# A written order for the start of a transformer layer, V weights a trip earlier, and one mixed tile on other engines

## The chip, the cores and the metric

The kernel runs on one core of one Trainium2 chip. TensorE (PE in the profile) multiplies matrices, ScalarE (ACT), VectorE (DVE) and GpSimd (POOL) work elementwise, and SyncE (SP) issues most of the transfers. The metric is the device time of one execution in microseconds (us), lower is better, compared as medians of several runs.

## The reference, cut to what matters

One decoder layer on x (1024 x 1024, float32). The change touches the first lines, where the groups' projection is made, and a split of the mixed result.

```
h = rms_norm(x, norm_mix_pre)
proj = h @ w_in                     # 1024 x 2816: u, v (256 each), q, k, vb (768 each)
a_out = spatial_gating(u, v, ...)   # gelu, LayerNorm of v in 4 groups, 128x128 causal w_s per group
b_out = dilated_attention(q, k, vb) # 12 heads
x = x + rms_norm(concat(a_out, b_out) @ w_out, norm_mix_post)
x = x + rms_norm(conv_gated_mlp(rms_norm(x, norm_ffn_pre)), norm_ffn_post)
```

## The kernel before, in words

All matmuls are made in pairs of reduced-precision parts. `split` (L71) copies a float32 block into a high part (`hi`, on ScalarE, VectorE or POOL) and subtracts that from the block to get the low part (`lo`); a product is then three matmuls: high by high, high by low, low by high.

The stages follow each other: the uv stage (normalise x, transpose it, project it on the u and v columns and gate), the V stage (projection on the attention's V columns in two halves, v0 and v1), the attention with 12 heads, the output projection, and the gated MLP.

The uv stage is a loop over eight tiles of 128 tokens (L329), here called trips 0 to 7. Its parts:

- `load_x` (L177) and `load_w` (L184) issue transfers on SP. x has two buffers, so the load of tile i+2 waits until tile i is normalised. The V weights use the two buffers called raw (L122), which `rows` and `spr` hold first.
- `norm_x` (L199): ScalarE squares a tile with a running sum (L212), POOL makes the mean `n_m` and the reciprocal root `n_r` (L145, L147), VectorE multiplies into `xn` (L214). Tile 0 goes in two halves, and takes the gain `g1` from two PSUM banks, into which TensorE spreads its one row (L253); the later tiles take it from `g1t` in SBUF, a copy by ScalarE (L259).
- `trans_x` (L217): TensorE transposes eight 128 x 128 blocks of `xn` into two PSUM banks; from each, ScalarE makes two high parts hTh and VectorE two low parts hTl.
- `split_w` (L190) splits a block of weights, `whuv`, `wluv` for u and v, and `whv`, `wlv` for V.
- `proj_a` (L234): 24 matmuls for a tile, three for each of eight blocks k. After k = 3 (after k = 5 for tile 0) it calls `mid`, which transposes the next tile, and finishes parts of earlier tiles.
- the gate in pieces, so that a tile's gate is spread over three trips: `uv_a` (L289: two Gelu on ScalarE; sum, mean, difference on VectorE; square on POOL, L300), `uv_b` (L302: sum of squares `s` on VectorE, `ln_m` and `ln_r` on POOL), `uv_c` (L308: product with `ln_r` on VectorE, product and sum with the gains `lnt` on POOL, L311, L312), `uv_d` (L314: split into vnh on ScalarE and vnl on VectorE).
- at the end of trip 1, `trans_rows` (L271) transposes `rows`; at the end of trip 2, `spatial_prep` (L320) masks `spr` on POOL (L321), transposes it on TensorE into spT (L325), and copies it to `wT`.

What sets the order: TensorE and SP issue their instructions as the code is written (`tc.manual_schedule(engines={ET.PE, ET.SP})`, L92). For ScalarE, VectorE and POOL a planner with a model of costs chooses the order at build time. In trip i the code has, in this order: `norm_x(i + 2)`, `load_x(i + 3)`, in trips 3 to 6 a load and a split of V weights (L342 to L344, low part on POOL), `proj_a(i)` with `mid` inside (`trans_x(i + 1)`, `uv_b(i - 1)`, `uv_d(i - 2)`), `uv_a(i)`, `uv_c(i - 1)`, and then the two preparations.

In the attention, `qk_row` (L510) makes the scores of 128 queries: TensorE, VectorE (L523), ScalarE's Exp (L528), a reciprocal `rz` (L530), and POOL's scaling of the row (L531). `tpv` (L538) transposes rows, splits them into pth (ScalarE) and ptl (VectorE, L556), and multiplies by V (L573). `load_qk` (L447) splits a head's weights, the low part wql on POOL. In the last head but one, `mix_split` (L614) splits seven blocks of the first tile of the mixed result, called `ms`, for the output projection: blocks with odd k by ScalarE and POOL, those with even k by VectorE alone.

Of the kernel before, what the change touches and what calls it, by code (L numbers as in the profile page):

```python
# [62 lines left out]
def build(tc, x, g1, g2, g3, g4, w_in, ln_g, ln_b, sp_w, sp_b, rel, w_out, w_gate, w_up,  # L63
# [7 lines left out]
    def split(hi, lo, src, hi_eng, lo_eng):  # L71
        if hi_eng is act:
            act.activation(hi, src, AF.Copy)  # L73
        elif hi_eng is pool:
            pool.tensor_scalar(hi, src, 1.0, None, op0=OP.mult)
        else:
            dve.tensor_copy(hi, src)
        lo_eng.tensor_sub(lo, src, hi.bitcast(F))  # L78
# [10 lines left out]
    def close_pool(key):  # L89
        cms.pop(key).__exit__(None, None, None)  # L90

    with tc.manual_schedule(engines={ET.PE, ET.SP}), \  # L92
# [17 lines left out]
        def bO(nm):  # L110
            return bank("O", 1, nm)
# [7 lines left out]
        def mtile(nm, dt=F):  # L119
            return mp.tile([128, 1024], dt, tag="M", name=nm)  # L120
# [8 lines left out]
        make_identity(nc, ident)  # L129
        half = cp.tile([128, 1], F, name="half")  # L130
        pool.memset(half, -0.5)
        ones = cp.tile([1, 128], F, name="ones")
        pool.memset(ones, 1.0)
        rows = raw("rows")
# [42 lines left out]
        def load_x(i):  # L177
            xt = sxp.tile([128, D], F, tag="x", name="x%d" % i)
            w = 512 if i == 0 else D
            for c in range(0, D, w):  # L180
                sp.dma_start(xt[:, c:c + w], x[i * 128:(i + 1) * 128, c:c + w])
            XT[i] = xt

        def load_w(key, c0, n, kp):  # L184
            r = mtile("r%d" % kp) if key == "uv" else raw("w%s%d" % (key, kp))
            v = r[:, :2 * n].rearrange("p (k c) -> p k c", k=2)
            sp.dma_start(v, w_in[kp * 256:(kp + 1) * 256, c0:c0 + n].rearrange("(k p) c -> p k c", p=128))
            RAW[key, kp] = v
# [25 lines left out]
                dve.scalar_tensor_tensor(xn, xt, r, g1t, op0=OP.mult, op1=OP.mult)  # L214
            XT[i] = xn

        def trans_x(i):  # L217
            if i == 0:
                for hf in range(2):
                    for kp in range(4):  # L220
                        for w in range(2):
                            hT[hf, kp, w] = htile("hT%s%d_%d" % ("hl"[w], hf, kp)).rearrange("p (k c) -> p k c", k=2)
            xn = XT[i]
            for q in range(2):
                p = bS("xT%d_%d" % (i, q))
                for k in range(4):
                    pe.transpose(p[:, k * 128:(k + 1) * 128], xn[:, (4 * q + k) * 128:(4 * q + k + 1) * 128], ident)
                s = slice((i % 4) * 128, (i % 4 + 1) * 128)
                for j in range(2):
                    pv = p[:, j * 256:(j + 1) * 256].rearrange("p (k c) -> p k c", k=2)  # L230
                    hi, lo = hT[i // 4, 2 * q + j, 0][:, :, s], hT[i // 4, 2 * q + j, 1][:, :, s]
                    split(hi, lo, pv, act, dve)

        def proj_a(key, n, i, nm, mid=None):  # L234
            p = bD(nm)
# [8 lines left out]
                pe.matmul(p[:, :n], hTv(i, k, 1), wh, start=False, stop=k == KT - 1)  # L244
            return p

        g1t, g1r = mtile("g1t"), mtile("g1r")
        load_x(0)
        sp.dma_start(g1r[0:1, :], bass.AP(tensor=g1.tensor, offset=g1.offset, ap=[[D, 1], [1, D]]))
        G1 = [bP("g1_%d" % hf) for hf in range(2)]  # L250
        for hf in range(2):
            s = slice(hf * 512, (hf + 1) * 512)
            pe.matmul(G1[hf], ones, g1r[0:1, s], start=True, stop=True)  # L253
        for kp in range(4):
            load_w("uv", 0, 512, kp)
        load_x(1)
        norm_x(0)
        for hf in range(2):
            act.activation(g1t[:, hf * 512:(hf + 1) * 512], G1[hf], AF.Copy)  # L259
        split_w("uv", 512, 0, dve, dve)  # L260
        trans_x(0)
        for kp in range(1, 4):
            split_w("uv", 512, kp, act if kp % 2 else dve, dve)

        def load_rows():
            sp.dma_start(rows[0:66, 0:128], conv_w.rearrange("k (f p) -> (k f) p", p=128))
# [53 lines left out]
        def spatial_prep():  # L320
# [5 lines left out]
            act.activation(wT[:, 0:512], p, AF.Copy)  # L326
            dve.tensor_sub(wT[:, 512:1024], p, wT.bitcast(F)[:, 0:512])

        for i in range(NT):  # L329
            if i == 0:  # L330
                load_x(2)
                norm_x(1)
            if i + 2 < NT:
                norm_x(i + 2)
            if i + 3 < NT:
                load_x(i + 3)
            if i == 0:
                sp.dma_start(lnt[:, 0:256], bcast(ln_g, 256))
                sp.dma_start(lnt[:, 256:512], bcast(ln_b, 256))
                sp.dma_start(sprv, sp_w.rearrange("g t s -> t g s"))  # L340
                load_rows()
            if i in (3, 4, 5, 6):  # L342
                load_w("v0", C0["v"], 384, i - 3)
                split_w("v0", 384, i - 3, act, pool)  # L344
            def mid():
                if i + 1 < NT:
                    trans_x(i + 1)
                if i >= 1:
                    uv_b(i - 1)
                if i >= 2:  # L350
                    uv_d(i - 2)

            p = proj_a("uv", 512, i, "uv%d" % i, mid)
            uv_a(i, p)
            if i >= 1:
                uv_c(i - 1)
            if i == 1:
                trans_rows()
            if i == 2:
                spatial_prep()  # L360
        close_pool("sx")

        BB = []
# [247 lines left out]
                split(wh[:, s], wl[:, s], r[:, s], ENG[WO_HI[k]], ENG[WO_LO[k]])  # L611
            WO.append((wh, wl))

        def mix_split(i, mh, ml, ks):  # L614
            s = slice(i * 128, (i + 1) * 128)
            for k in ks:
                src = mixT[k][:, s]
                split(mh[:, k], ml[:, k], src, act if k % 2 else dve, pool if k % 2 else dve)
            MS[i] = (mh, ml)

        YP = {}
# [18 lines left out]
        for h in range(HEADS):  # L640
            if h + 1 < HEADS:
                load_bias(h + 1)
            if h + 2 < HEADS:
                load_qk(h + 2)
            if h + 3 < HEADS:
                bias_copies(h + 3)
            if h == HEADS - 1:
                pump(len(fill))
                fill.extend(wout_mm(0, range(KT - 1), bD))
            for g in range(4):  # L650
                if g < 3:
                    qk_group(h, g + 1)
                elif h + 1 < HEADS:
                    qk_group(h + 1, 0)
                if h == HEADS - 2:
                    if g == 0:
                        m0 = [mtile("ms0_%d" % s, R).rearrange("p (k c) -> p k c", k=KT) for s in range(2)]
                        mix_split(0, m0[0], m0[1], range(KT - 1))
                    for k in WO_AT[g]:
                        load_wo(k)  # L660
                if h == 0 and g == 0:
                    pump(FILL_FIRST)
                last_pv()
                last_pv = tpv(h, g, FILL_AT.get(h, FILL)[g])
                if g == 3 and h + 2 < HEADS:
                    fill.extend(proj_qk(h + 2))
                if g == 3 and h == HEADS - 2:
                    pump(len(fill))
                    for k in WO_AT[4]:
                        load_wo(k)  # L670
# [586 lines left out]
```

## Time and profile before

| what | value |
|---|---|
| runs | 1202.24, 1201.06, 1197.48 us; median 1201.06 |
| the profiled execution's own time | 1199.82 us |
| its span, first to last instruction | 1198.1 us |
| mean granted TensorE clock | 0.992 of full speed |
| uv stage's last matmul issued | 71.46 us |
| first matmul of the V stage | 71.69 us |

In the rows of the profile, a line begins with its start and its length in us, or with a source line; then follow engine, operation, and out<-in by the program's names, the shape, and in brackets the idle time ahead of it and what ended that. `x4` is a count of instructions. A group's line ends with its busy time in us, the mean of one in ns, and the idle time before it. In the table of windows, the clock is the share of full speed that was granted to TensorE; at 0.50 its matmuls take twice the time.

### The profile page before, as it was taken

Reading aid. Unit: us, or ns where it says so; the run is one execution under the profiler, and the core shown is the slowest. Engines: PE = TensorE matmul, PEld = TensorE weight load, DVE = VectorE, ACT = ScalarE, POOL = GpSimd, SP = SyncE. Lnnn points to the kernel's source line nnn. Section 1 sums busy time; section 2 is a strip of 40 time slices with the busy share of each in tenths; the row PEclk is TensorE's granted clock in tenths of the full one; section 3 lists DMA queues with packets and bytes.
Section 4 is the critical chain, followed back from the end, with each engine's and each line's share of the span. In section 5 each row is a group of like instructions: output and inputs, shape, how many; then the busy total and the mean of one; then the engine's idle time right before and its main releaser. Section 6 shows DMA issues by size and latency. Waiting matters only on the chain.

```text
span 1198.1 us, 16554 instructions
## 1 busy us (share of the span) xinstructions
PE 1163.6 (97%) x5691; PEld 976.8 (82%) x5691; DVE 839.7 (70%) x1559; ACT 582.9 (49%) x1174; POOL 370.6 (31%) x402
## 2 busy tenths in 40 slices
PE   7899999999999999999999999999999999999996
PEld 5789978888887878887788888888888888888884
DVE  5752257777777775468997678777777679779665
ACT  5532256667765664457534243432434345446521
POOL 2850023334323374234033313332133310000451
PEclk9999999999999999999999999999999999999998
DMA  5323133343233442251143323433143289334345
GB/s 180 106 59 89 25 83 73 91 117 84 73 78 76 108 141 71 92 173 53 36 132 97 115 67 117 132 97 106 62 132 106 88 302 357 97 97 129 110 130 203
DMA packets 107420, 134.31 MB, mean 112 GB/s; under 512 B 30779, under 2 KB 74311, under 8 KB 107336
## 3 DMA queue, kind: packets, MB, share of 16 engines
q1 hardware_dynamic: 105032, 131.15, 35.9%
q10 hardware_dynamic: 2304, 2.10, 0.5%
q8 instruction: 45, 0.74, 0.3%
q14 instruction: 39, 0.32, 0.1%
HBM read 98.30 MB, written 35.71 MB: 112 GB/s over the span
## 4 chain that ended last, share of the span: by engine, by line
PE 86%; DVE 5%; DMA 3%; POOL 2%; ACT 2%; issue 2%; SPq 0%; DVEq 0%; POOLq 0%; ACTq 0%
PE d L996 15%; PE qk L479 10%; PE y L630 7%; PE o L573 4%; PE pt L551 4%; PE s L519 2%; PE s L520 2%; PE v L242 2%; PE v L244 2%; PE v L243 2%; PE Bu L857 2%; PE Au L856 2%; PE Au L857 2%; PE Au L855 2%; PE Bu L856 2%; PE Bu L855 2%
## 5 line engine op out<-in xcount | busy, mean ns | idle before, releaser
L996 PE MATMUL d<-t,s 128*128 128x512 f32 x924 | 211.9, 391 | 1.9 <-ACT t L73 1.6
L996 PEld LDWEIGHTS d<-t,s 128*128 128x128 f32 x924 | 174.5, 189 | 39.2 <-ACT t L73 2.0
L531 POOL TENSOR_SCALAR row<-row,rz 128x128 f32<-128x128 f32 (+3 forms) x96 | 72.8, 759 | 213.2 <-DVE rz L530 200.2
L528 ACT ACTIVATE row<-row,nm 128x128 f32<-128x128 f32 (+3 forms) x96 | 74.4, 775 | 49.0 <-DVE nm L523 48.7
L556 DVE TENSOR_TENSOR ptl<-pt,pth 128x512 fp32r<-128x512 f32 (+1 forms) x120 | 75.7, 634 | 19.6 <-ACT pth L555 18.3
L630 PE MATMUL y<-woh,ms 128*128 128x512 f32 x256 | 82.8, 396 | 0.4 <-DVE Q L494 0.4
L555 ACT ACTIVATE pth<-pt 128x512 fp32r<-128x512 f32 (+1 forms) x120 | 65.8, 550 | 33.3 <-PE pt L551 31.9
L479 PE MATMUL qk<-hTh,wqh 128*128 128x512 f32 x192 | 81.1, 422 | 0.0
L73 ACT ACTIVATE s<-sf 128x512 fp32r<-128x512 f32 x77 | 48.2, 626 | 65.7 <-PE d L996 26.4
L479 PE MATMUL qk<-hTl,wqh 128*128 128x512 f32 x192 | 78.7, 410 | 0.0
L479 PE MATMUL qk<-hTh,wql 128*128 128x512 f32 x192 | 76.6, 399 | 0.0
L78 DVE TENSOR_TENSOR s<-sf,s 128x512 fp32r<-128x512 f32 x77 | 53.5, 695 | 24.0 <-ACT s L73 23.9
L551 PE MATMUL pt<-ident,row 128*128 128x128 f32 x432 | 68.4, 274 | 1.6 <-POOL row L531 1.5
L1011 POOL TENSOR_TENSOR x<-x,g4t 128x512 f32<-128x512 f32 x12 | 18.4, 1536 | 158.0 <-DMA g4t<-in_norm_ffn_post 133.8
L73 ACT ACTIVATE wtg<-tg 128x512 fp32r<-128x512 f32 x44 | 27.5, 632 | 80.9 <-PE Cu L857 67.8
L805 POOL TENSOR_TENSOR tu<-wu 128x512 f32<-128x512 f32 x11 | 17.5, 1590 | 156.1 <-PE Ag L857 74.5
L908 DVE SCALAR_TENSOR_TENSOR c<-G,cols,c 128x1023 f32<-128x1023 f32 (+1 forms) x44 | 57.7, 1329 | 6.7 <-ACT c L906 6.7
L523 DVE CUSTOM_DVE_ANT_0 row<-s,bias 128x384 f32<-128x384 f32 (+2 forms) x96 | 49.9, 519 | 17.7 <-PE s L520 11.8
L551 PEld LDWEIGHTS pt<-ident,row 128*128 128x128 f32 x432 | 51.3, 140 | 10.4 <-POOL row L531 2.5
L73 ACT ACTIVATE wtu<-tu 128x512 fp32r<-128x512 f32 x44 | 27.6, 630 | 64.2 <-PE Cg L857 50.8
L630 PEld LDWEIGHTS y<-woh,ms 128*128 128x128 f32 x256 | 47.9, 188 | 10.8 <-issue 0.8
L573 PE MATMUL o<-ptl,V 128*128 128x256 f32 x240 | 49.4, 287 | 4.8 <-DVE ptl L556 4.5
(329 smaller groups left out, 3232.5 us busy)
## 6 DMA issues: line engine op xcount, KB each, us to landing
sf<-sD SPq DMA_DIRECT2D x77, 256.0 KB, 2.8
wu<-in_w_up SPq DMA_DIRECT2D x11, 1024.0 KB, 5.0
wd<-in_w_down SPq DMA_DIRECT2D x22, 512.0 KB, 7.0
wg<-in_w_gate SPq DMA_DIRECT2D x10, 1024.0 KB, 6.0
sD<-c SPq DMA_DIRECT2D x30, 256.0 KB, 6.5
gcop<-gd SPq DMA_DIRECT2D x12, 576.0 KB, 4.8
wqk<-in_w_in SPq DMA_DIRECT2D x24, 256.0 KB, 6.0
bias<-gcop SPq DMA_DIRECT2D x12, 512.0 KB, 4.1
```

The costliest lines, as they stand in the source:

```text
L73: act.activation(hi, src, AF.Copy)
L78: lo_eng.tensor_sub(lo, src, hi.bitcast(F))
L479: pe.matmul(st[hf], w, m, start=k == 0 and j == 0, stop=k == KT - 1 and j == 2)
L528: act.activation(t[:, :w], t[:, :w], AF.Exp, bias=nm, scale=-1.0, accum_out=z)
L531: pool.tensor_scalar(t[:, :w], t[:, :w], rz, 1.0, op0=OP.mult, op1=OP.mult)
L551: pe.transpose(p[:, a * 128:(a + 1) * 128], r[:, jj * 128:(jj + 1) * 128], ident)
L555: act.activation(hi[:, :n], p[:, :n], AF.Copy)
L556: dve.tensor_sub(lo[:, :n], p[:, :n], hi.bitcast(F)[:, :n])
L573: pe.matmul(ov, v, t[:, s], start=j == 0 and x == 0, stop=x == 1 and j == 2 * g + 1, skip_group_check=True)
L630: pe.matmul(YP[i, hf], m, w, start=k == 0 and j == 0, stop=k == KT - 1 and j == 2)
L908: dve.scalar_tensor_tensor(c[:, d:T], g[:, 0:T - d], col(2 - d, f), c[:, d:T], op0=OP.mult, op1=OP.add)
L996: pe.matmul(b, l, r, start=first and n in FIRST and q == 0, stop=last and n in LAST and q == 2, skip_group_check=True)
```

## The change

Five things are changed.

1. From the first loads to the end of the uv loop, ScalarE, VectorE and POOL are put under a written order as well: each issues its instructions as the code has them.
2. The start is written anew for that: the gain's row is loaded from ScalarE's queue, ahead of x; the four weight loads and the load of tile 1 come directly behind the load of tile 0; the first tile's normalisation comes ahead of the first weight split; the weight splits have ScalarE for all high parts, and the second of them stands between the two halves of the first tile's transposes; the copies of the gain come after the third; `norm_x(1)` moves up from trip 0.
3. TensorE multiplies a tile of zeros three times ahead of the gain's matmuls (`wz`, cleared by VectorE, into the bank `bO`).
4. The V weights are loaded in trips 2 to 5. They are split at the end of `mid` in trips 3, 4, 6 and 7, the low part on POOL in trips 3 and 4 and on VectorE in trips 6 and 7.
5. The seven blocks of the first mixed tile are all split by ScalarE and POOL.

```
+        wz = cp.tile([128, 256], F, name="wz")
+        dve.memset(wz, 0.0)
...
-        def trans_x(i):
+        def trans_x(i, mid=None):
...
+                if q == 0 and mid is not None:
+                    mid()
...
+        order = tc.manual_schedule(engines={ET.DVE, ET.Activation, ET.Pool})
+        order.__enter__()
         g1t, g1r = mtile("g1t"), mtile("g1r")
+        wb = bO("wb")
+        act.dma_start(g1r[0:1, :], bass.AP(tensor=g1.tensor, offset=g1.offset, ap=[[D, 1], [1, D]]))
         load_x(0)
-        sp.dma_start(g1r[0:1, :], bass.AP(tensor=g1.tensor, offset=g1.offset, ap=[[D, 1], [1, D]]))
+        for kp in range(4):
+            load_w("uv", 0, 512, kp)
+        load_x(1)
+
+        for _ in range(3):
+            pe.matmul(wb[:, :256], wz[:, :128], wz, start=True, stop=True)
         G1 = [bP("g1_%d" % hf) for hf in range(2)]
...
-        for kp in range(4):
-            load_w("uv", 0, 512, kp)
-        load_x(1)
         norm_x(0)
+        split_w("uv", 512, 0, act, dve)
+
+        def rest():
+            split_w("uv", 512, 1, act, dve)
+
+        trans_x(0, rest)
+        split_w("uv", 512, 2, act, dve)
         for hf in range(2):
             act.activation(g1t[:, hf * 512:(hf + 1) * 512], G1[hf], AF.Copy)
-        split_w("uv", 512, 0, dve, dve)
-        trans_x(0)
-        for kp in range(1, 4):
-            split_w("uv", 512, kp, act if kp % 2 else dve, dve)
+        split_w("uv", 512, 3, act, dve)
+        norm_x(1)
...
+        V0 = {3: 0, 4: 1, 6: 2, 7: 3}
         for i in range(NT):
             if i == 0:
                 load_x(2)
-                norm_x(1)
...
-            if i in (3, 4, 5, 6):
-                load_w("v0", C0["v"], 384, i - 3)
-                split_w("v0", 384, i - 3, act, pool)
+            if i in (2, 3, 4, 5):
+                load_w("v0", C0["v"], 384, i - 2)
             def mid():
...
+                if i in V0:
+                    split_w("v0", 384, V0[i], act, pool if i < 5 else dve)
...
+        order.__exit__(None, None, None)
         close_pool("sx")
...
-        def mix_split(i, mh, ml, ks):
+        def mix_split(i, mh, ml, ks, engs=None):
...
-                split(mh[:, k], ml[:, k], src, act if k % 2 else dve, pool if k % 2 else dve)
+                split(mh[:, k], ml[:, k], src, *(engs or ((act, pool) if k % 2 else (dve, dve))))
...
-                        mix_split(0, m0[0], m0[1], range(KT - 1))
+                        mix_split(0, m0[0], m0[1], range(KT - 1), (act, pool))
```

## The prediction

> **What bounds the kernel now.** I read the page's busy shares first, then the chain that ended last.
>
> ```profile
> PE 1163.6 (97%) x5691; PEld 976.8 (82%) x5691; DVE 839.7 (70%) x1559; ACT 582.9 (49%) x1174; POOL 370.6 (31%) x402
> PE 86%; DVE 5%; DMA 3%; POOL 2%; ACT 2%; issue 2%; SPq 0%; DVEq 0%; POOLq 0%; ACTq 0%
> ```
>
> TensorE is busy 97% of the span and carries 86% of the chain, so a change that leaves its matmuls alone can only move the places where it waits or runs at a lower clock. The table by windows shows two such places that the change touches (columns: stretch, its length, busy time of PE, PEld, DVE, ACT, POOL, then the granted clock):
>
> ```profile
> 41.42:47.91 6.49, 6.49 (x33) 5.34 (x32) 3.58 (x9) 4.48 (x11) 5.18 (x8) 1.00 0.61 203
> 47.91:51.86 3.95, 0.64 (x4) 0.19 (x2) 3.54 (x4) 0.70 (x3) 3.79 (x4) 1.00 0.14 23
> 53.12:56.53 3.41, 3.41 (x12) 2.81 (x11) 2.01 (x5) 1.93 (x4) 3.24 (x7) 0.50 0.01 2
> 56.53:71.69 15.16, 15.16 (x72) 12.36 (x71) 9.72 (x23) 5.02 (x15) 11.73 (x15) 1.00 0.23 67
> 367.40:370.57 3.17, 0.50 (x3) 0.50 (x4) 2.69 (x4) 1.55 (x4) 2.18 (x3) 1.00 0.14 31
> 370.57:373.97 3.40, 3.40 (x12) 2.82 (x11) 1.71 (x6) 0.59 (x1) 0.59 (x1) 0.50 0.05 11
> ```
>
> The first row is one dense trip of the uv loop, a projection and eight transposes: 6.5 us. In the second and the fifth TensorE stands (3.95-0.64 = 3.3 us, and 2.7 us), and soon after each it runs 3.4 us at half clock, which costs 3.4 x 0.5 = 1.7 us. The stalls are thus worth 5.0 and 4.4 us. After the second stretch the uv stage is dense to its end at 71.69 us (15.16 of 15.16). The timeline shows what made both stalls:
>
> ```profile
> 48.32 2.82 DVE L214 SCALAR_TENSOR_TENSOR xn<-x,n_6r,g1t 128x1024 f32<-128x1024 f32 x1 [0.49 <-ACT whv L73]
> 48.25 1.80 POOL L78 TENSOR_TENSOR wlv<-wv,whv 128x768 fp32r<-128x768 f32 x1
> 366.58 2.84 DVE L78 TENSOR_TENSOR ms<-mix,ms 128x128 fp32r<-128x128 f32 x3
> 366.62 2.65 POOL L78 TENSOR_TENSOR wql<-wqk,wqh 128x512 fp32r<-128x512 f32 x2 [0.17 <-ACT wqh L73]
> 370.07 0.50 PE L573 MATMUL o<-ptl,V 128*128 128x256 f32 x2 [2.68 <-DVE ptl L556]
> ```
>
> [...]
>
> **The change, step by step.** The V-weight splits go behind the transposes and later by an iteration, so 5.0 us of stall may go; the mixed tile leaves VectorE, so 4.4 us may go. But ScalarE, VectorE and POOL, which a planner orders now, get the order in which the code is written, and that order has to be followed through the loop. The rows for one trip:
>
> ```profile
> 33.22 1.28 DVE L214 SCALAR_TENSOR_TENSOR xn<-x,n_4r,g1t 128x1024 f32<-128x1024 f32 x1 [0.39 <-POOL n_4r L147]
> 39.93 1.28 DVE L214 SCALAR_TENSOR_TENSOR xn<-x,n_5r,g1t 128x1024 f32<-128x1024 f32 x1 [0.39 <-POOL n_5r L147]
> 39.02 0.25 POOL L145 TENSOR_SCALAR n_5m<-ss 128x1 f32<-128x1 f32 x1
> 39.35 0.55 POOL L147 TENSOR_TENSOR n_5r<-n_5m,half 128x1 f32<-128x1 f32 x1
> L78 DVE TENSOR_TENSOR hTl<-xT,hTh 128x256 fp32r<-128x256 f32 x28 | 11.0, 417 | 3.0 <-ACT hTh L73 2.7
> L73 ACT ACTIVATE hTh<-xT 128x256 fp32r<-128x256 f32 x28 | 10.1, 381 | 17.2 <-DVE hTl L78 11.1 <-PE xT L227 6.0
> 71.46 0.39 PE L244 MATMUL uv<-whuv,hTl 128*128 128x512 f32 x1
> 70.62 0.43 DVE L310 TENSOR_TENSOR tm<-tm,ln6r 128x256 f32<-128x256 f32 x1 [1.42 <-POOL ln6r L147]
> 71.13 0.73 POOL L311 TENSOR_TENSOR tm<-tm,lnt 128x256 f32<-128x256 f32 x1 [0.54 <-DVE tm L310]
> 71.94 0.74 POOL L312 TENSOR_TENSOR tm<-tm,lnt 128x256 f32<-128x256 f32 x1
> 73.53 0.73 POOL L300 TENSOR_TENSOR tm<-tm 128x256 f32<-128x256 f32 x1 [0.85 <-DVE tm L299]
> 74.29 0.42 DVE L305 TENSOR_REDUCE s<-tm 128x4 f32<-128x256 f32 x1 [0.51 <-POOL tm L300]
> 74.80 0.19 POOL L145 TENSOR_SCALAR ln7m<-s 128x4 f32<-128x4 f32 x1 [0.54 <-DVE s L305]
> 75.07 1.02 POOL L147 TENSOR_TENSOR ln7r<-ln7m,half 128x4 f32<-128x4 f32 x1
> 24.69 0.74 POOL L321 TENSOR_SCALAR_AFFINE_SELECT spr<-spr 128x512 f32<-128x512 f32 x1 [4.98 <-DMA spr<-in_spatial_w]
> 34.49 0.60 PE L325 MATMUL spT<-ident,spr 128*128 128x128 f32 x4
> 34.85 0.48 PE L242 MATMUL uv<-whuv,hTh 128*128 128x512 f32 x1
> ```
>
> Now the normalisations of tiles 4 and 5 are 6.71 us apart (33.22 to 39.93), and a trip of TensorE takes 6.5, so they keep step. Written out, trip i has on POOL: n_m, n_r of tile i+2; ln_m, ln_r of tile i-1; the square of tile i; the two lnt products of tile i-1. On VectorE: xn of tile i+2; four hTl of tile i+1; s of tile i-1; vnl; the three mean steps of tile i; the product with ln_r. This closes a loop that none of the two may overtake: xn (1.28) -> four hTl, two of which wait for a ScalarE hTh in between, which itself waits for the hTl before it (4 x 0.42 + 2 x 0.38 = 2.4) -> s (0.42) -> ln_m and ln_r (74.80 to 76.09: 1.3) -> product (0.43) -> square (0.73) -> two products (71.13 to 72.68: 1.6) -> n_m, n_r (39.02 to 39.90: 0.9) -> xn of the next tile. The sum is 9.1 us a trip where TensorE needs 6.5.
>
> *Start.* The rows:
>
> ```profile
> 1.68 0.33 SPq L249 DMA_DIRECT2D g1r<-in_norm_mix_pre  x1
> 17.75 1.28 DVE L214 SCALAR_TENSOR_TENSOR xn<-x,n_1r,g1t 128x1024 f32<-128x1024 f32 x1 [1.53 <-POOL n_1r L147]
> 14.76 0.63 PE L243 MATMUL uv<-wluv,hTh 128*128 128x512 f32 x1
> 16.33 0.39 PE L242 MATMUL uv<-whuv,hTh 128*128 128x512 f32 x1
> x<-in_x SPq DMA_DIRECT2D x4, 512.0 KB, 4.1
> 23.98 1.07 ACT L212 ACTIVATE xn<-x 128x1024 f32<-128x1024 f32 x1
> 26.96 1.31 DVE L214 SCALAR_TENSOR_TENSOR xn<-x,n_3r,g1t 128x1024 f32<-128x1024 f32 x1 [0.15 <-POOL n_3r L147]
> ```
>
> The gain's row is loaded from ScalarE's queue, ahead of its first square, for which it has to wait anyway; SP's queue then issues the first weights 0.33 us sooner. All four high parts go to ScalarE, two of them from VectorE, and the two engines pass blocks to and fro in a fixed order. I take 0 for xn of tile 1, now at 17.75, with bounds of -1 (VectorE has two copies less) and +2 (ScalarE has two more, and the two gain copies, ahead of tile 1's square). The three dummy matmuls are covered by the wait for the gain's row, without which TensorE has nothing to do; uncovered they would cost 2 to 4 us (three to six passes at the 0.63 below).
>
> At 14.76 a matmul takes 0.63 us, and at 16.33 it takes 0.39. [...]
>
> *Trips 1 and 2.* xn of tile 3 comes at 27 as now: its load needs the buffer that xn of tile 1 leaves at 19.03, takes 4.1, and ScalarE's square at 23.98 follows. Then xn of tile 4 comes at 27.0+9.1 = 36.1, not 33.2. TensorE isn't held yet: tile 3 is transposed already, and projection 2 ends near 35. But behind it stand, in TensorE's own written order, the four spT transposes, and they wait for POOL's masking of spr. Now POOL does it at 24.69, when it is idle; written, it comes last in trip 2. Its place follows from xn of tile 4: 36.1 + 1.28 + 2.4 + 0.42 + 1.3 + 0.43 + 0.73 + 1.6 = 44.3, masking 0.74 and the transposes 0.4: projection 3 starts near 45.6, and not at 34.85. That is **+10.7 us**. It has a floor, if nothing lags: from the last matmul of a tile (71.46) to the end of its square (74.26) it is 2.8 us, then 1.6 and 0.74: 5.1, of which TensorE stands 4.9.
>
> *Clock.* A stand of 3.3 us brought 3.4 us at half clock; one of 10 us meets a clock that is down already, and stays down for one to two such stretches: 1.7 to 3.4. I take **+2.2**.
>
> *Trips 3 to 6.* ScalarE's square for tile 5 stands behind the copy of spT (about half a square's 1.07), and n_m, n_r (0.9) follow, so xn of tile 5 comes near 45.6+0.5+1.1+0.3+0.9 = 48.4. In trips 3 and 4 POOL has a V-weight part more (1.80 above), which makes a loop of 9.1+1.8 = 10.9: xn of tile 6 at 59.3, of tile 7 at 70.2. TensorE: projection 3 from 45.6 with the slow clock to 54.3, projection 4 to 60.8, projection 5 needs hTl of tile 5, which stands behind xn of tile 6 (59.3+1.28+0.42 = 61.0): in time, near enough; it ends at 67.5. Projection 6 needs hTl of tile 6 at its third matmul, behind xn of tile 7: 70.2+1.7 = 71.9; it stands **4 us**, and once more the clock falls (**1.7**). It ends near 67.5+6.5+4+1.7 = 79.7; projection 7 has no transposes (6.5 less twice the 0.36 that four take between 34.49 and 34.85, 5.8): 85.5. The last V part, on VectorE in trip 7, comes late for the third pair of V blocks: 0.7. That is 86.2 against 71.69: **+14.5**. The 5.0 us that leave are in this already, as I compare ends. Bounds: with the floor alone 4.9+1.7-5.0 = +1.6; with POOL and VectorE blocking each other more, +20.
>
> *Loads.* SP issues the V loads a trip sooner. The second needs spr's buffer, which the late spT frees only near 46, and x of tile 7 stands behind it on SP's queue: 46+4.1 is still 20 us ahead of xn of tile 7, which covers it; without that cover it would cost up to the 4.1.
>
> [...]
>
> *Mixed tile.* VectorE loses four copies and four differences; ScalarE gets four more copies, POOL four more differences.
>
> ```profile
> 365.15 1.30 POOL L78 TENSOR_TENSOR ms<-mix,ms 128x128 fp32r<-128x128 f32 x3
> ```
>
> That is 4 x 0.43 = 1.7 us on POOL, and on ScalarE under 4 x 0.38 = 1.5 (hTh has twice the columns). The stall of 2.7 and its 1.7 of slow clock go; next late is POOL, which has seven differences (3.0) and two wql (2.65) in a row ahead of the rows' scaling: up to 1.7 back. Bounds -4.4 to +1; I take **-3.5**, as the stall's cause (three differences of VectorE behind wql) is gone.
>
> **Sum.** +14.5 - 3.5 = +11.0 on the profiled execution's own 1199.82 us (span 1198.1, 1.7 around it; the runs' median is 1201.06): 1210.8 us.
>
> ```profile
> 60.00:200.00 140.00, 138.06 (x761) 124.19 (x760) 60.74 (x173) 55.87 (x140) 36.36 (x43) 1.00 0.28 69
> ```
>
> Behind the uv stage TensorE's work is dense (138.06 of 140 us), so little absorbs the shift. 0.5%, about what a measurement here can tell, is 6 us.
>
> **Rivals.** (a) POOL is nowhere behind: the masking costs its floor (4.9 and 1.7), the old stall (5.0) goes, the tile gives 3.5: 1199.82+1.6-3.5 = 1197.9, no change. It needs a loop under 6.5 us, which decides; against it the 9.1 summed from rows, for it that a planner could hide the same work. Chance 0.11. (b) The written order doesn't reach POOL's place for the masking (it still runs near 25 us, when spr lands): the two stalls go and nothing comes in: 1199.82-5.0-3.5 = 1191.3, faster. The change would not do what it says; nothing in the profile speaks for it, but TensorE's rows at 34.49 and 34.85 do show a written order being kept (spT just ahead of projection 3). Chance 0.06. (c) As forecast, but the scaled rows wait behind the mixed tile on POOL and give all of the 3.5 back: 1214.3. Chance 0.18; forecast proper 0.65.
>
> **Numbers.** The forecast 1210.8 is the likeliest; the range reaches from (a), with part of what lies between, to the bound of +20 for the loop: 1199 to 1220. Slower by over 0.5% has the forecast and (c): 0.82; within 0.5% (a) and a little: 0.11; faster 0.07.
>
> **What would show it.** Right: the masking of spr near 45 us with the spT transposes right behind it and TensorE idle from about 35; xn of tiles 4, 6 and 7 some 9 to 11 us behind the one before; granted clock 0.50 near 46 and again near 75; V projection from about 86; no stall at 367. Wrong: spr before 36 us, xn rows 6.5 us apart, or V projection starting before 75.

## The result, and the profile after

The kernel after takes 1211.2 us (median of 4 runs, 1210.63 to 1212.13), the kernel before 1200.9 us (4 runs on the same chip). The ratio is 1.0100, with a 95% interval of 1.0086 to 1.0114: 12 us slower by the ratio, 10.3 by the medians. The forecast was 1210.8.

The busy shares on the page of after hardly differ from those of before (TensorE 97% in both):

```profile
span 1209.4 us, 16562 instructions
PE 1169.0 (97%) x5697; PEld 979.7 (81%) x5697; DVE 836.0 (69%) x1552; ACT 584.5 (48%) x1180; POOL 365.7 (30%) x404
PE 84%; DVE 5%; POOL 3%; ACT 2%; DMA 2%; issue 2%; SPq 0%; DVEq 0%; POOLq 0%; ACTq 0%
```

The span is 11.3 us longer (1209.4 against 1198.1). Of these, 5.4 us are busy TensorE (1169.0 against 1163.6, with the same matmuls but for six passes over zeros): 2.9 us are the passes over zeros, made while TensorE would otherwise wait for the gain's row, and the other 2.5 are put down to slower clock (an estimate: between 16 and 400 us TensorE works 11.8 us at half clock, against 6.8 in before, and half of the difference is 2.5). The rest is standing still, that is, waiting. Totals don't say where. For that, set each matmul beside the same matmul of before (TensorE's order is the same in both) and see where the distance changes:

| the same matmul | before, us | after, us | later by |
|---|---|---|---|
| first transpose of tile 1 | 19.09 | 19.75 | 0.7 |
| a matmul of projection 1 | 22.59 | 24.86 | 2.3 |
| first spT transpose | 34.49 | 45.56 | 11.1 |
| a late matmul of projection 3 | 39.78 | 53.15 | 13.4 |
| projection 5, behind before's first stand | 58.39 | 68.15 | 9.8 |
| projection 6, third matmul | 60.03 | 73.76 | 13.7 |
| first matmul of the V stage | 71.69 | 87.06 | 15.4 |
| last matmul ahead of before's second stand | 367.12 | 382.26 | 15.1 |
| a matmul soon behind it | 378.06 | 389.49 | 11.4 |

Everything is lost in the first 87 us, and 3.7 us come back near 370. The rows of after that answer to those shown of before, from the table by windows (length; PE, PEld, DVE, ACT, POOL busy; granted clock):

```profile
36.94:45.56 8.62, 0.00 (x1) 0.00 (x1) 5.20 (x11) 1.89 (x6) 3.92 (x6) 0.69 0.19 61
45.56:50.31 4.75, 4.75 (x13) 3.88 (x14) 1.72 (x2) 1.63 (x3) 0.73 (x2) 0.50 0.28 85
69.95:73.76 3.81, 0.00 (x0) 0.00 (x0) 1.62 (x2) 0.02 (x1) 1.86 (x4) 1.00 0.41 121
74.20:77.60 3.40, 3.40 (x10) 2.57 (x9) 2.72 (x8) 1.44 (x5) 1.31 (x3) 0.53 0.13 28
77.60:87.06 9.46, 9.46 (x46) 7.73 (x45) 6.07 (x14) 3.84 (x10) 6.81 (x11) 0.99 0.17 46
```

TensorE stands 8.6 us and then runs at half clock; it stands 3.8 us and again runs at half clock; from 77.6 on it is dense. At half clock the loop's 512-column matmuls start 0.43 us apart (21.94 and 22.37), at full clock 0.23 (23.46 and 23.69): 1.8 times, not quite twice. The timeline of after, first the rows of POOL, VectorE and TensorE around the masking, then those of a trip with a V part:

```profile
36.37 0.55 POOL L149 TENSOR_TENSOR n_4r<-n_4m,half 128x1 f32<-128x1 f32 x1
36.95 1.28 DVE L216 SCALAR_TENSOR_TENSOR xn<-x,n_4r,g1t 128x1024 f32<-128x1024 f32 x1 [2.38 <-POOL n_4r L149]
40.56 0.41 DVE L320 TENSOR_REDUCE s<-tm 128x4 f32<-128x256 f32 x1
41.06 0.30 POOL L147 TENSOR_SCALAR ln1m<-s 128x4 f32<-128x4 f32 x1 [4.14 <-DVE s L320]
44.19 0.72 POOL L327 TENSOR_TENSOR tm<-tm,lnt 128x256 f32<-128x256 f32 x1
44.87 0.64 POOL L336 TENSOR_SCALAR_AFFINE_SELECT spr<-spr 128x512 f32<-128x512 f32 x1
45.56 1.11 PE L340 MATMUL spT<-ident,spr 128*128 128x128 f32 x4 [8.62 <-POOL spr L336]
49.28 1.28 DVE L216 SCALAR_TENSOR_TENSOR xn<-x,n_5r,g1t 128x1024 f32<-128x1024 f32 x1 [1.25 <-POOL n_5r L149]
52.16 0.42 DVE L78 TENSOR_TENSOR hTl<-xT,hTh 128x256 fp32r<-128x256 f32 x1 [1.59 <-ACT hTh L73]
56.44 1.89 POOL L78 TENSOR_TENSOR wlv<-wv,whv 128x768 fp32r<-128x768 f32 x1
56.55 2.06 DVE L325 TENSOR_TENSOR tm<-tm,ln2r 128x256 f32<-128x256 f32 x1
58.29 0.79 POOL L315 TENSOR_TENSOR tm<-tm 128x256 f32<-128x256 f32 x1
61.53 1.29 DVE L216 SCALAR_TENSOR_TENSOR xn<-x,n_6r,g1t 128x1024 f32<-128x1024 f32 x1 [2.92 <-POOL n_6r L149]
72.09 1.28 DVE L216 SCALAR_TENSOR_TENSOR xn<-x,n_7r,g1t 128x1024 f32<-128x1024 f32 x1 [2.89 <-POOL n_7r L149]
73.76 0.50 PE L248 MATMUL uv<-whuv,hTl 128*128 128x512 f32 x1 [3.82 <-DVE hTl L78]
```

Read it as a chain in which each engine stands for the other. VectorE is idle 2.38 us for `n_4r`, makes xn and the hTl, and only then `s`; for that POOL has stood 4.14 us; POOL's last step of the trip is the masking, and for that TensorE has stood 8.62. Neither POOL nor VectorE is full: in the 8.62 us they are busy 3.92 and 5.20. Their orders interlock.

### The profile page after: what moved, and what is told of

It is laid out like the page before. It is cut to its first block, busy times and chain, and to the rows that moved or that the text cites. A ratio compares the mean times of both kernels' runs of the same rounds, so it can differ in the third digit from the quotient of the medians.

```text
span 1209.4 us, 16562 instructions
## 1 busy us (share of the span) xinstructions
PE 1169.0 (97%) x5697; PEld 979.7 (81%) x5697; DVE 836.0 (69%) x1552; ACT 584.5 (48%) x1180; POOL 365.7 (30%) x404
## 4 chain that ended last, share of the span: by engine, by line
PE 84%; DVE 5%; POOL 3%; ACT 2%; DMA 2%; issue 2%; SPq 0%; DVEq 0%; POOLq 0%; ACTq 0%
PE d L1014 15%; PE qk L497 10%; PE y L648 7%; PE o L591 4%; PE pt L569 4%; PE v L246 2%; PE s L537 2%; PE v L248 2%; PE v L247 2%; PE Bu L875 2%; PE Au L875 2%; PE Au L873 2%; PE Au L874 2%; PE Bu L873 2%; PE Bu L874 2%
## 5 line engine op out<-in xcount | busy, mean ns | idle before, releaser
L546 ACT ACTIVATE row<-row,nm 128x128 f32<-128x128 f32 (+3 forms) x96 | 74.4, 775 | 50.3 <-DVE nm L541 47.8
L574 DVE TENSOR_TENSOR ptl<-pt,pth 128x512 fp32r<-128x512 f32 (+1 forms) x120 | 75.6, 634 | 19.8 <-ACT pth L573 18.7
L823 POOL TENSOR_TENSOR tu<-wu 128x512 f32<-128x512 f32 x11 | 17.5, 1593 | 156.0 <-PE Ag L875 74.4
L541 DVE CUSTOM_DVE_ANT_0 row<-s,bias 128x384 f32<-128x384 f32 (+2 forms) x96 | 49.8, 519 | 17.5 <-PE s L538 11.8
L648 PEld LDWEIGHTS y<-woh,ms 128*128 128x128 f32 x256 | 47.9, 188 | 10.9 <-issue 0.8
```

Of the source, the lines that this page charges most:

```text
L546: act.activation(t[:, :w], t[:, :w], AF.Exp, bias=nm, scale=-1.0, accum_out=z)
L574: dve.tensor_sub(lo[:, :n], p[:, :n], hi.bitcast(F)[:, :n])
L648: pe.matmul(YP[i, hf], m, w, start=k == 0 and j == 0, stop=k == KT - 1 and j == 2)
```

## The experiments

Each comparison is with runs of the kernel before on the same chip, and ratios are to it. Its median was 1201.0 us for the first four experiments below (to the early masking), 1199.5 for the normalisation ahead, the V parts on VectorE, the run without dummies and the first candidate, and 1199.2 for the others.

**The mixed tile alone.** Before, with the change's new argument of `mix_split` and this call:

```
-                        mix_split(0, m0[0], m0[1], range(KT - 1))
+                        mix_split(0, m0[0], m0[1], range(KT - 1), (act, pool))
```

> The kernel before with the mixed tile's seven blocks on ScalarE and POOL alone. Theory A (the low parts ms of VectorE were held by POOL's wql, and ptl behind them held TensorE): the wait of 2.7 us at 370 and the 3.4 us at half clock behind it go, so 4.4 us less: about 1195.4 for the 1199.8 of the profiled execution, and no clock step near 370. Rival (POOL's seven differences hold up the scaled rows instead): 0 to 2 us less, with TensorE waiting for the scaled row near 370.

1195.95 us, 0.9958 (0.9947 to 0.9969): 5.0 us faster by the ratio. The stand near 370 is gone. The timeline of this run shows POOL's differences in a row (six of the seven are in the trace), and `ptl` at its 0.69 us beside them:

```profile
366.34 2.58 POOL L78 TENSOR_TENSOR ms<-mix,ms 128x128 fp32r<-128x128 f32 x6
367.48 0.69 DVE L556 TENSOR_TENSOR ptl<-pt,pth 128x512 fp32r<-128x512 f32 x1 [0.69 <-ACT pth L555]
368.40 0.39 PE L573 MATMUL o<-ptl,V 128*128 128x256 f32 x2
369.77 2.56 POOL L78 TENSOR_TENSOR wql<-wqk,wqh 128x512 fp32r<-128x512 f32 x2
```

The wql parts now come after the mixed tile's, where TensorE no longer waits for what stands beside them. This part of the change is a gain by itself.

**No written order.** After, without these lines (ScalarE, VectorE and POOL go back to the planner):

```
-        order = tc.manual_schedule(engines={ET.DVE, ET.Activation, ET.Pool})
-        order.__enter__()
...
-        order.__exit__(None, None, None)
```

> The changed kernel without the written order on ScalarE, VectorE and POOL; all else stays (new start, zeros' matmuls, V loads and splits moved, mixed tile). Theory A (the written order on POOL and VectorE makes the uv stage longer): the masking of spr is back near 25 us, the V stage begins at 67 to 72 us and not at 87, and the time is 1190 to 1196. Rival B (the new start and the moved V loads cost the time): the V stage begins after 80 us, and the time stays over 1205.

1198.1 us, 0.9985 (0.9972 to 0.9998). Against after's 1.0100 the written order costs 0.0115, or 13.8 us; the time is still above the 1190 to 1196 expected. The masking is back at 24.86 us and the spT transposes at 34.66; the V stage starts at 71.36. But before's first stand is not gone, though the V weights come a trip sooner and the code has their split behind the transposes:

```profile
49.28 0.95 DVE L78 TENSOR_TENSOR wlv<-wv,whv 128x768 fp32r<-128x768 f32 x1
50.67 1.28 DVE L216 SCALAR_TENSOR_TENSOR xn<-x,n_6r,g1t 128x1024 f32<-128x1024 f32 x1 [0.44 <-POOL n_6r L149]
52.68 0.51 PE L248 MATMUL uv<-whuv,hTl 128*128 128x512 f32 x1 [2.54 <-DVE hTl L78]
```

**The written order for the start alone.** After, with the order's end ahead of the loop:

```
         norm_x(1)
+        order.__exit__(None, None, None)
...
-        order.__exit__(None, None, None)
```

> The changed kernel, with the written order ended ahead of the uv loop; the start up to the normalisation of tile 1 keeps it. Theory A: the start's order costs under 1 us and the loop's order all of the rest: within 2 us of the run without any written order. Rival B (the start costs, by its clock): 3 us or more slower than that run, with matmuls of 0.63 us at 22 us.

1198.01 us, 0.9978 (0.9968 to 0.9988), the same as without any written order. So the start's order costs and brings nothing that these runs can tell; it is the loop's order that costs. The rival's sign did show, half clock from 19.4 to 22.8 us in the profile, but not its 3 us.

**The masking early.** After, with the masking taken out of `spatial_prep` into a function of its own, called in trip 1; all else in the written order:

```
             if i + 2 < NT:
                 norm_x(i + 2)
+            if i == 1:
+                spatial_mask()
```

> The changed kernel, with the masking of spr written behind POOL's n_m and n_r in trip 1 and not at the end of trip 2; the rest of the written order stays. Theory A (two things: the masking's place, and the loop of 9 to 10 us over POOL and VectorE): TensorE's 8.6 us wait for spT goes, but the loop then ends later projections, and of the 11 us only about half comes back: the V stage begins at 81 to 83 us (87.1 in the changed kernel), 1205 to 1207. Rival C (the masking's place is all of it): the V stage begins at 75 to 77 us, 1199 to 1201.

1207.38 us, 1.0061 (1.0040 to 1.0083), the V stage at 82.66. TensorE's stand of 8.6 us is gone; three others take its place. The rows are of VectorE's xn and of TensorE:

```profile
37.62 1.29 DVE L216 SCALAR_TENSOR_TENSOR xn<-x,n_4r,g1t 128x1024 f32<-128x1024 f32 x1 [2.42 <-POOL n_4r L149]
46.56 1.28 DVE L216 SCALAR_TENSOR_TENSOR xn<-x,n_5r,g1t 128x1024 f32<-128x1024 f32 x1 [1.97 <-POOL n_5r L149]
57.12 1.28 DVE L216 SCALAR_TENSOR_TENSOR xn<-x,n_6r,g1t 128x1024 f32<-128x1024 f32 x1 [2.93 <-POOL n_6r L149]
67.70 1.28 DVE L216 SCALAR_TENSOR_TENSOR xn<-x,n_7r,g1t 128x1024 f32<-128x1024 f32 x1 [2.93 <-POOL n_7r L149]
37.94 0.60 PE L342 MATMUL spT<-ident,spr 128*128 128x128 f32 x4
48.24 0.51 PE L248 MATMUL uv<-whuv,hTl 128*128 128x512 f32 x1 [2.18 <-DVE hTl L78]
58.80 0.51 PE L248 MATMUL uv<-whuv,hTl 128*128 128x512 f32 x1 [2.21 <-DVE hTl L78]
69.38 0.50 PE L248 MATMUL uv<-whuv,hTl 128*128 128x512 f32 x1 [2.25 <-DVE hTl L78]
```

The distances are 8.9, 10.6 and 10.6 us, where the prediction summed 9.1 and 10.9 from rows of before. That the masking is all of the loss is refuted: without its wait 7.3 of the 12 us stay. A TensorE that does not stand for the masking catches up with the chain and stands for the chain.

**The normalisation ahead of the two lnt products.** The kernel with the early masking, with `norm_x(i + 3)` written at the end of trip i ahead of `uv_c(i - 1)`, instead of `norm_x(i + 2)` at the start of trip i. The masking stands behind `norm_x(3)` again.

```
-            if i + 2 < NT:
-                norm_x(i + 2)
-            if i == 1:
-                spatial_mask()
+            if i == 0:
+                norm_x(2)
...
             uv_a(i, p)
+            if i + 3 < NT:
+                norm_x(i + 3)
+            if i == 0:
+                spatial_mask()
```

> The kernel after, with the masking of spr early and each normalisation written ahead of the two lnt products instead of behind them; nothing else differs. Theory A (the 9.1 us of a trip are the sum of the written chain over POOL and VectorE): the two products (1.5 us) leave the chain, and the product with ln_r (0.43) goes behind xn, so xn of tiles 4 and 5 come 7 to 7.5 us behind the one before, of tiles 6 and 7 one V part later (8.9 to 9.3); TensorE's waits for hTl, 2.2 us each in the run with the early masking, are under 1 us; the V projection starts at 75 to 77 us, and the time is 1200 to 1202. Rival (the trip is set by how busy POOL and VectorE are and by their blocking each other, not by the order): the spacing stays at 9 to 9.2 and the V projection at 82 to 83, the time at 1207.

1200.67 us, 1.0009 (0.9998 to 1.0020), the V stage at 77.30.

```profile
35.44 1.28 DVE L216 SCALAR_TENSOR_TENSOR xn<-x,n_4r,g1t 128x1024 f32<-128x1024 f32 x1 [1.95 <-POOL n_4r L149]
42.98 1.29 DVE L216 SCALAR_TENSOR_TENSOR xn<-x,n_5r,g1t 128x1024 f32<-128x1024 f32 x1 [1.68 <-POOL n_5r L149]
52.80 1.28 DVE L216 SCALAR_TENSOR_TENSOR xn<-x,n_6r,g1t 128x1024 f32<-128x1024 f32 x1 [3.21 <-POOL n_6r L149]
62.02 1.28 DVE L216 SCALAR_TENSOR_TENSOR xn<-x,n_7r,g1t 128x1024 f32<-128x1024 f32 x1 [3.21 <-POOL n_7r L149]
```

7.5 us, then 9.8 and 9.2 with the V parts: the same instructions with one step moved take 1.4, 0.7 and 1.4 us less a trip, and the whole is 6 us faster. This shows that the order makes the trip's length and not the amount of work. The waits did not all go under 1 us as expected: three of them together are still 6.1 us, the longest 2.5.

**V parts on VectorE.** The kernel with the early masking, and:

```
-                    split_w("v0", 384, V0[i], act, pool if i < 5 else dve)
+                    split_w("v0", 384, V0[i], act, dve)
```

> The kernel after, with the masking of spr early and all low parts of the V weights on VectorE (after has the first two on POOL); nothing else differs. Theory A (a V part on POOL lengthens the chain of its trip by its 1.8 us): xn of tiles 6 and 7 come 9.0 to 9.2 us behind the one before instead of 10.6, two of TensorE's three waits of 2.2 us get shorter, the V projection starts 2 to 3 us sooner than with the early masking alone (79.5 to 80.5), time 1204 to 1205. Rival (VectorE is just as much on the chain, so the part costs the same there): spacing 10.3 to 10.8, V projection at 82 to 83, 1207.

1205.0 us, 1.0038 (1.0024 to 1.0052), the V stage at 80.56. The last two distances are 9.5 (46.5 to 56.01, and on to 65.55) instead of 10.6. The gain is 1.0 a trip and not the 1.5 expected; POOL's small `ln2r` now meets VectorE's part (0.96 us from 50.79) and takes 1.65 us here, from 50.97, instead of 1.02. The interval of the ratio overlaps that of the early masking alone, so the gain is read from the distances and not from the time.

**The repairs together.** The early masking, the normalisation first, and the V parts on VectorE, by the edits above.

> The kernel after with the masking early, each normalisation ahead of the two lnt products, and all low parts of the V weights on VectorE: the three repairs of the written order together. Theory A (the repairs add up, since each takes its own term from the chain): xn 7.3 to 8 us apart in all trips, V projection at 74.5 to 76, time 1198 to 1200. Rival (VectorE now sets the trip, with V parts of 1.2 us on it): spacing 8.5 or more in the trips with V parts, V projection at 77 or later, 1200.5 or more.

1198.25 us, 0.9995 (0.9985 to 1.0006), the V stage at 73.99, a little sooner than expected. The xn of tiles 4 to 7 come at 35.6, 43.1, 52.0 and 60.2: the distances of 8.8 and 8.3 are over the 8 expected. The interval touches that of the normalisation ahead with POOL's V parts (0.9998 to 1.0020), so what the V parts add there is not clear of noise. The written order is now level with before; but the mixed tile's 5 us are in it: without them it would, by the first experiment's size, still be slower.

**POOL's order alone, and the other two alone.** After, first with one engine and then with the other two in the written order:

```
-        order = tc.manual_schedule(engines={ET.DVE, ET.Activation, ET.Pool})
+        order = tc.manual_schedule(engines={ET.Pool})
```

```
-        order = tc.manual_schedule(engines={ET.DVE, ET.Activation, ET.Pool})
+        order = tc.manual_schedule(engines={ET.DVE, ET.Activation})
```

> The kernel after, but only POOL keeps the written order; ScalarE and VectorE are ordered by the planner again. Nothing else differs. Theory A (two causes: POOL's place for the masking, and the chain over POOL and VectorE, which the planner can shorten by the part that lies on VectorE): the masking still stands behind the two lnt products of trip 2, but s of tile 1 need not wait for tile 2's four hTl, so the spT transposes start at 40 to 42 us instead of 45.6 (floor: projection 2's end near 35 plus 5.1), the spacing of the normalisations falls to 7 to 8, the V projection starts at 77 to 80, time 1201 to 1204. Rival (POOL's order alone makes it all): transposes at 45 or later, V projection at 85 or later, 1209 or more.

1202.65 us, 1.0033 (1.0020 to 1.0046), the V stage at 78.42. The masking came at 42.52, later than expected, and the rest as expected but for one thing: the xn are not closer (10.2, 11.2 and 9.6 us apart), and yet TensorE does not wait for hTl in these trips. The planner puts xn behind hTl that TensorE needs sooner, so the same lateness of xn holds up nobody. The spacing is thus no measure by itself; what stands behind xn on VectorE is.

> The kernel after, but POOL is ordered by the planner again; ScalarE and VectorE keep the written order. Nothing else differs. The planner then puts the masking behind tile 2's statistics, and each n_m (of later tiles n_r too) between the two lnt products. Theory A: no wait of TensorE at the spT transposes (they start near 38 instead of 45.6); the normalisations 8.2 to 8.6 us apart at first (9.1 less one product), 9.5 to 10 in the trips with V parts; V projection at 79.5 to 81.5, time 1203 to 1206. Rival (VectorE's written order alone makes the 9.1): spacing and V projection as with the early masking (9.0 to 10.6, 82.7), 1207.

1204.25 us, 1.0046 (1.0029 to 1.0064), the V stage at 81.42, all as expected. The masking is early (26.11); the distances are 8.8 (a little over the 8.6 expected), 9.6 and 10.0. Over the 0.9985 without written order, POOL's order costs 0.0048 and the order of the other two 0.0061, together 0.0109 of the 0.0115 that all three cost: POOL's side of the interlocked pair and the other side are worth about half each. ScalarE's order was not separated from VectorE's.

**No dummy matmuls.** After, without the zero tile and its three matmuls:

```
-        for _ in range(3):
-            pe.matmul(wb[:, :256], wz[:, :128], wz, start=True, stop=True)
```

> The kernel after without its zero tile and the three dummy matmuls. Theory A (tile 1's normalisation ends the start, not TensorE's matmuls): xn of tile 1 and the spT transposes stay within 0.5 us of where after has them, and the time within 2 us of 1211; only the granted clock of the first 8 us changes. Rival (the dummies warm TensorE and so gain up to the 4.3 us of the first 18 matmuls): 1213 to 1216, everything from tile 1 on later.

1211.1 us, 1.0093 (1.0077 to 1.0108), the same as after. (The rival's 4.3 us is an estimate from two rows of before: 18 matmuls, each shorter by the step from 0.63 us at 14.76 to 0.39 at 16.33.) xn of tile 1 starts at 18.8 instead of 18.41, the V stage at 86.47 instead of 87.06. The dummies bring nothing that can be measured; why is seen further down.

**Two candidates under the planner.** First before, with the mixed tile of the change and the V parts' low parts on VectorE; then after without written order and with the low parts on VectorE. The first one's second edit:

```
-                split_w("v0", 384, i - 3, act, pool)
+                split_w("v0", 384, i - 3, act, dve)
```

> The kernel before with two edits: the first mixed tile by ScalarE and POOL (part of the change), and the low parts of the V weights on VectorE instead of POOL, all under the planner. Theory A (before's stand at 50 us comes of VectorE's xn blocked by POOL's V part of 1.8 us): without that POOL instruction xn of tile 6 takes 1.3 instead of 2.8, TensorE's stand of 2.5 to 3.3 us near 50 goes below 1.5 and the V projection starts at 67 to 70 instead of 71.7: 1191 to 1194. Rival (the planner only shifts VectorE's load, and hTl stands behind a V part on VectorE itself): the stand stays at 2 us or more, 1195 to 1198.

1194.9 us, 0.9963 (0.9950 to 0.9976), not told apart from the mixed tile alone (0.9958). TensorE still stands 1.69 and 1.09 us near 51 and 54, and the V stage starts at 70.99. That lies between theory and rival, and does not decide.

> The kernel after with the written order taken off all three engines and the low parts of the V weights on VectorE alone; the loads and splits of the V weights stand where after writes them, and the mixed tile is by ScalarE and POOL. A candidate for the best. Theory A (the stand near 50 us comes of a V part ahead of a tile's xn and hTl, on whichever of the two engines): TensorE's stand near 50 is 1 to 2 us instead of the 2.5 under the planner with POOL's parts, V projection at 69.5 to 71, time 1193.5 to 1196.5, as in the run of before with the two edits (1194.9). Rival (POOL's part was not in the way): V projection 71.4 and 1198, as with POOL's parts.

1192.64 us, 0.9945 (0.9933 to 0.9958), the lowest ratio of all: 6.5 us faster than before and 4.8 faster than the same kernel with POOL's parts (0.9985). Its interval overlaps that of the mixed tile alone (0.9947 to 0.9969), so a gain beyond that of the tile is not shown by the time. Time and V stage (68.92) are a little better than the theory expected. The table by windows of this run:

```profile
41.42:60.00 18.58, 17.94 (x87) 14.16 (x86) 15.73 (x34) 9.77 (x25) 14.11 (x18) 1.00 0.27 84
60.00:68.92 8.92, 8.92 (x43) 7.28 (x41) 5.78 (x14) 3.04 (x8) 6.48 (x10) 1.00 0.28 89
```

Its timeline around tile 6, of TensorE, VectorE and POOL:

```profile
44.02 0.50 PE L248 MATMUL uv<-whuv,hTl 128*128 128x512 f32 x1 [0.64 <-DVE hTl L78]
50.08 1.28 DVE L216 SCALAR_TENSOR_TENSOR xn<-x,n_6r,g1t 128x1024 f32<-128x1024 f32 x1
50.30 1.93 POOL L149 TENSOR_TENSOR ln3r<-ln3m,half 128x4 f32<-128x4 f32 x1
51.28 0.75 DVE L78 TENSOR_TENSOR hTl<-xT,hTh 128x256 fp32r<-128x256 f32 x2
```

TensorE is busy 17.94 of 18.58 us where before it stood 3.3 and slowed down; xn of tile 6 takes its undisturbed 1.28. Neither the weights a trip earlier nor the low part on VectorE does this alone (the stand is 2.54 with the first, 1.69 and 1.09 with the second; the planner makes another order in each of these kernels).

## Why the prediction was right, point by point

**The masking and its place** were right to the step: the prediction had the masking near 44.3 and projection 3, behind masking and transposes, from 45.6 on. The masking came at 44.87, the transposes at 45.56 and projection 3 at 46.33, 11.5 us later than in before where 10.7 were forecast. This also rules out rival (b), a masking that stays near 25 us. The chain from xn of tile 4 to the masking was summed as 8.2 us (36.1 to 44.3) and took 7.9 (36.95 to 44.87); that it was shorter made up in part for an xn that was late.

**The start** is the term that was mis-sized. It was put at 0, with bounds of -1 and +2, and measured +2.3 at projection 1: 0.7 for xn of tile 1 (18.41 against 17.75), as bounded, and 1.6 of half clock between 19.8 and 23.2 us, which the prediction had not thought of. The dummies were said to cost nothing, covered by the wait for the gain's row; the run without them shows that. In after the step to full clock comes sooner: matmuls take 0.40 us from 13.2 on, where in before one still takes 0.63 at 14.76. How much of that the dummies did, and how much the new start, was not shown. But a stand of 2.51 us, up to 19.75, takes it back, and the time does not change; the forecast has no gain from it, rightly.

**The clock** behind the long stand: +2.2 forecast, 2.3 measured (11.1 to 13.4); the clock fell at 40.3, within the stand, and came back at 50.5. Behind the second stand: 1.7 forecast, 1.6 measured (13.73 to 15.37).

**The loop** of 9.1 us, and 10.9 with a V part, was measured as 8.9 and 10.6 in the run without the masking's wait. In after itself xn of tile 6 came 12.3 us behind that of tile 5 and not 10.9: VectorE stood 1.59 us for tile 4's hTh, whose transposes came only at 51.11, behind the slow half of projection 3. So tile 6 was 2.2 late (61.53 against 59.3), projection 5, called in time, stood 1.3 us, and projection 6 stood 3.8 where 4 were said.

**The third V part**, put at 0.7 late on VectorE, was not: TensorE is dense from 77.60 to 87.06. V stage: +14.5 forecast, +15.4 measured, the 2.3 of the start being more than the difference. Not all of the 2.3 lasts to there: the run without dummies, which kept full clock at the start, has its V stage only 0.6 us sooner.

**The loads** cost nothing, as said: ScalarE's square for tile 7 runs at 66.24, behind its other work, without a wait for a transfer.

**VectorE beside POOL.** In before the normalisation of tile 6 takes 2.82 us beside POOL's V part of 1.80, against 1.28 elsewhere, and hTl, for which TensorE waits until 51.86, stands behind it (from 51.39). After has the like: VectorE's product takes 2.06 us beside the V part of 1.89 (56.55 and 56.44), where the product of tile 6 in before took 0.43. Not every pair does this: in before VectorE's difference `tm` at 53.58 keeps its 0.42 us beside POOL's `ln3r` (53.12 to 54.14), and hTl at 51.72 its 0.41 beside a V part (51.26 to 53.16). In after it cost nothing: what the long product delays on VectorE was waiting for POOL in the loop anyway. The product ends at 58.61, and POOL takes it up at 59.05, behind its own square. The bound of +20, for more of this, had no row under it; the V stage came 15.4 us later.

**The mixed tile**: -3.5 forecast, -3.7 in the profile of after (15.1 to 11.4), -5.0 as a change by itself. Rival (c), that POOL's scaled rows wait behind it, did not come: behind the second stand's place TensorE waits 0.47 us. Rival (a), a POOL that is nowhere behind, would need a trip under 6.5 us; from tile 4 on none of the written orders came under 7.3.

**Where the reasoning was too simple.** The sum treats the masking (+10.7) and the chain as terms to be added. The runs show that they overlap: taking the masking out gives back 4.4 us of the V stage's start and 3.9 thousandths of the time, 4.7 us, not 10.7, because a TensorE that comes sooner to the chain waits for that. The sum was still right, since it followed both along one line of time. That it came within 0.4 us of the median is partly luck: the start's 2.3 us and the third V part's 0.7 lie on opposite sides, and the runs of before alone spread over 4.8 us.

What stays open in part: why the kernel without written order (0.9985) is not as fast as the mixed tile alone (0.9958), although its V stage starts 1.6 us sooner in the profiles (71.36 against 72.93). The runs of the two spread over 4.6 and 2.5 us, and the profiles are from opposite ends of that. The first is of the fastest run of its kernel (1195.99 us, median 1198.1), in which the stand of 2.54 us left the clock full. The second is of the slowest (1197.16, median 1195.95): the first weights came 1.1 us later than in before (VectorE's first split starts at 8.16 and not at 7.06), though every engine has the same order as in before up to the V stage, and that stage starts 1.2 us later (72.93 against 71.69). So a single profile places the V stage only to within 1 or 2 us.

## What to carry to other kernels

Before an order is written out by hand, write down for each engine of a pair what the two hand each other in one trip, and add up the closed path: if the sum (here 9.1 us) is longer than the bound engine's trip (6.5), the order can lose, however idle both engines look, and moving one step (here the normalisation ahead of two products) can give back more than moving work to another engine does: 6 us here, against 3 at most for the V parts under the written order. A step with no hurry by its own data, like the masking, belongs where its engine is idle, and not where its consumer is written. When a wait is removed, look for the next chain behind it before its whole length is booked as gain.

## What the runs showed of the hardware that was not expected

**A stand of 2.5 us may cost the clock or not.** With the dummies TensorE stood 2.51 us ahead of tile 1's transposes and then ran 3.4 us at half clock; without them it stood 2.50 us there and kept full clock. From the table by windows of after, the stretch that ends where the clock falls, and the slow one behind it:

```profile
16.38:19.79 3.41, 0.90 (x5) 0.41 (x3) 2.51 (x2) 2.11 (x5) 1.90 (x3) 1.00 0.00 0
19.79:23.20 3.41, 3.41 (x12) 3.05 (x13) 2.34 (x4) 1.04 (x3) 0.55 (x1) 0.50 0.67 203
```

The same columns for the run without dummies, over the two stretches that hold the stand:

```profile
15.00:18.40 3.40, 2.10 (x8) 1.05 (x6) 2.34 (x2) 3.40 (x6) 0.42 (x2) 1.00 0.00 0
18.40:21.80 3.40, 1.70 (x12) 1.57 (x13) 2.32 (x2) 0.83 (x3) 2.04 (x3) 1.00 0.20 35
```

In after the clock changes at 19.8, 23.2, 40.3, 50.5, 74.4 and 77.8 us, all apart by multiples of about 3.41. If TensorE is judged by fixed stretches of that length, the stand fell into one stretch in after (busy 0.90 of 3.41) and over two in the other run (2.10 and 1.70 of 3.40). The traces of before and after bear this out. In each, all changes of the clock lie whole multiples of 3.413 us apart, from a point that differs between the two. From 12 us on, TensorE was busy for at most 0.46 of every full-clock stretch behind which the clock was halved (1.56 of 3.41 us from 1172.70 in before), and for at least 0.62 of every one behind which it was kept (2.12 of 3.41 from 60.75 in after). It is a reading of the traces; no run moved a stand across such a border on purpose. Nearly the same stand thus cost 1.6 us at half clock in after and no clock in the run without dummies. The length of a stand alone does not tell: 2.51 us in after and 2.18 in the run with the early masking were enough, and the latter's matmuls take 0.63 us from 49.58 on; behind 2.54 us in the run without written order they go on at 0.39 and 0.40 (53.02 to 53.95).

**POOL's smallest instructions are held up as well.** `ln3r` on 128x4 takes 1.02 us in after and 1.93 beside VectorE's xn in the second candidate (50.30 to 52.23, through VectorE's instruction of 50.08 to 51.36). Moving the V parts off POOL shortened the trips here (9.5 us instead of 10.6 with the early masking), but POOL's short steps beside VectorE's long ones grew, from 1.02 us to 1.65 and 1.93.
